# A rebuilt opening for a three-block network: shift by TensorE, x in eight pieces, four small loads on ScalarE's queue

## The chip, the cores and the metric

The kernel is one program on one core of a Trainium2 chip. The metric is the device time of one execution in microseconds (us). The kernel before took 3019.31 us as the median of three runs (3010.18 to 3040.72).

## The reference

A token matrix x (512 tokens x 1024) goes through two layers of a conditioned block and then a third block. The change is in the first microseconds of the first layer:

```
mod = silu(c) @ w_ada[0] + b_ada[0]            # c: 1 x 1024, w_ada: 1024 x 6144
sh1, sc1, g1, sh2, sc2, g2 = split(mod, 6)     # 1024 values each
h = rmsnorm(x, mix_norm[0]) * (1 + sc1) + sh1
proj = h @ w_in                                # q, k, v: 3 x 1024 columns, forget gate: 16 columns
q = rmsnorm(q per head, q_norm);  k = rmsnorm(k per head, k_norm)
log_f = log_sigmoid(f_logit + b_f);  cum = cumsum(log_f)
attention with logits + cum[t] - cum[s], output projection, x = x + g1 * y, then a mixture of experts
```

rmsnorm divides each token by the root of its mean square and multiplies by a gain. The first projection needs all 1024 features of h, so it needs sh1 and sc1, and with them 2 x 1024 columns of w_ada: 8.4 MB of weights.

## The kernel before

x is held with features on the 128 partitions: x[:, c, :] is feature block c (of 8) for all 512 tokens. Products of high precision are made from pairs: a tensor is rounded to a high part (whi, h_hi) on ScalarE, the remainder (wlo, h_lo) is formed on VectorE or GpSimd, and three matmuls (lines 124 to 126) add up hi*hi, hi*lo and lo*hi. weight (line 108) loads a 128x1024 block of weights on SyncE's queue and makes that pair; four raw blocks are kept, so the next load waits for a remainder.

The opening (first_mod, line 274) does the first modulation. The weights w_ada0 are stored transposed, so that one block of 128x1024 gives 128 entries of mod: it is multiplied by silu(c), which stands in all 128 partitions, and summed along the row. The generator ada (line 156) does that for the sixteen blocks of scale and shift, alternating scale c and shift c: ten on VectorE in one instruction (line 182), six as a multiply on GpSimd (line 179) and a summing copy on ScalarE (line 168). Beside it ScalarE squares the eight blocks of x (line 285), VectorE adds the squares (line 287), four matmuls with a column of ones sum over the partitions (line 211), VectorE forms the inverse root (lines 139 to 144), and four matmuls spread it over the partitions (line 197). Then, block by block, VectorE makes a = (1 + scale) * gain and the scaled tile n_t = x * a * r (line 299), and spread (line 236) adds the shift and makes h_hi and h_lo, on changing engines.

After it, rope_tables (line 564) makes a table of sines, and fox_heads (line 449) runs the projections: groups of 24 matmuls of 256 columns into one of two accumulators, each followed by a square on ScalarE (qk_sq) and by a row sum and the multiplication with the gain of q or k on VectorE (qk_ss, qk_raw). fox_cum (line 403) runs beside the first group: 24 matmuls for the forget gate, then a chain on ScalarE. The other 32 column blocks of mod follow as work on the side (ada again), one by one beside the attention. A scheduler puts the instructions of each engine in an order before the program runs, by its own estimates; each engine then goes through its list strictly in that order and waits where an input is missing. [...]

Of the kernel before, what the change touches and what calls it, by code (L numbers as in the profile page):

```python
# [25 lines left out]
class Net:  # L26
# [247 lines left out]
    def first_mod(self, x, gain, c, w, mod, hp, pool):  # L274

        nc = self.nc
        V = nc.vector
        h = [hp.tile([128, 8, 512], F32R, tag=n, bufs=1, name=n) for n in ("h_hi", "h_lo")]
        self.ring = pool
        ada = self.ada(c, w, mod, [k for c in range(8) for k in (8 + c, c)], "VVSVVSVS", 8, 1)  # L280
        mod, _ = mod
        acc = pool.tile([128, T], F32, name="n_acc")
        for c in range(8):
            q = pool.tile([128, T], F32, tag="n_sq", bufs=3, name="n_sq") if c else acc
# [8 lines left out]
        for c in range(8):
            for _ in range(2):
                next(ada, None)
            a = self.small([128, 1], "fm_a", bufs=4)
            V.scalar_tensor_tensor(a, mod[:, 8 + c:9 + c], 1.0, gain[:, c:c + 1], op0=OP.add, op1=OP.mult)
            t = pool.tile([128, T], F32, tag="n_t", bufs=3, name="n_t")
            V.scalar_tensor_tensor(t, x[:, c, :], a, rb, op0=OP.mult, op1=OP.mult)
            self.spread(t, mod[:, c:c + 1], h[0][:, c, :], h[1][:, c, :], c)  # L300
        self.ring = None
        return h
# [100 lines left out]
    def fox_cum(self, h, cq, ck, room, keep):  # L403
# [45 lines left out]
    def fox_heads(self, h, oT, keep, pool):  # L449
# [3 lines left out]
        gq = pool.tile([128, 64], F32, name="fox_gq")  # L453
        gk = pool.tile([128, 64], F32, name="fox_gk")
        nc.sync.dma_start(out=gq, in_=A["fox_q_norm"].to_broadcast([128, 64]))
        nc.sync.dma_start(out=gk, in_=A["fox_k_norm"].to_broadcast([128, 64]))
# [1851 lines left out]
```

## Time and profile before

| | us |
|---|---|
| median of three runs | 3019.31 |
| lowest, highest | 3010.18, 3040.72 |
| profiled execution | 3015.39 |
| its span | 3013.6 |
| TensorE busy | 2731.0 (91%) |
| VectorE busy | 2345.1 (78%) |
| ScalarE busy | 1388.6 (46%) |
| GpSimd busy | 1230.1 (41%) |

A timeline row gives the start of a piece of work in us, its duration in us, the engine, the line, the operation, out<-in by the program's names, shapes, the number of instructions merged in the row, and in brackets the idle time of the engine before it and what ended it. PE is TensorE, DVE VectorE, ACT ScalarE, POOL GpSimd, SPq the queue on which SyncE issues DMAs. The ends of matmuls are modelled; their starts tell their pace. A float32 matmul leaves two records. [...]

### The profile page before, as it was taken

Reading aid. Unit: us, or ns where it says so; the run is one execution under the profiler, and the core shown is the slowest. Engines: PE = TensorE matmul, PEld = TensorE weight load, DVE = VectorE, ACT = ScalarE, POOL = GpSimd, SP = SyncE. Lnnn points to the kernel's source line nnn. Section 1 sums busy time; section 2 is a strip of 40 time slices with the busy share of each in tenths; the row PEclk is TensorE's granted clock in tenths of the full one; section 3 lists DMA queues with packets and bytes.
Section 4 is the critical chain, followed back from the end, with each engine's and each line's share of the span. In section 5 each row is a group of like instructions: output and inputs, shape, how many; then the busy total and the mean of one; then the engine's idle time right before and its main releaser. Section 6 shows DMA issues by size and latency. Waiting matters only on the chain.

```text
span 3013.6 us, 42664 instructions
## 1 busy us (share of the span) xinstructions
PE 2731.0 (91%) x14989; PEld 2229.8 (74%) x14989; DVE 2345.1 (78%) x4500; ACT 1388.6 (46%) x2672; POOL 1230.1 (41%) x894
## 2 busy tenths in 40 slices
PE   2999979897889798899898899999999999999996
PEld 1887556686546566577676588999999999998885
DVE  7999457858885685677974699998588888887667
ACT  3355437734554573532333533588633333333332
POOL 3111017733211573004941245120177777774442
PEclk9999779999899799999998999999999999999998
DMA  6766159934555796321011124696699999998882
GB/s 214 247 225 223 66 190 307 344 107 130 157 165 209 227 336 210 98 67 29 4 60 58 62 91 129 208 315 245 212 369 355 351 355 361 356 335 298 267 275 99
DMA packets 235778, 629.51 MB, mean 209 GB/s; under 512 B 33340, under 2 KB 97388, under 8 KB 232088
## 3 DMA queue, kind: packets, MB, share of 16 engines
q1 hardware_dynamic: 135856, 436.51, 42.8%
q0 software_dynamic: 45120, 154.42, 14.6%
q10 hardware_dynamic: 54568, 35.66, 4.0%
q8 instruction: 122, 2.00, 0.3%
q14 instruction: 112, 0.92, 0.1%
HBM read 565.93 MB, written 64.36 MB: 209 GB/s over the span
## 4 chain that ended last, share of the span: by engine, by line
PE 48%; DVE 13%; DMA 2%; issue 1%; ACT 1%; POOL 0%; POOLq 0%; SPq 0%; DVEq 0%; ACTq 0%
PE acc L124 7%; PE acc L125 7%; PE acc L126 7%; PE y L126 6%; PE y L125 6%; PE y L124 6%; DVE s_y L1375 1%; PE S L1930 1%; PE tr L1930 1%; DMA wraw<-in_moe_w_gu_dram 1%; DVE wlo L118 1%; DVE s_y L1534 1%; DMA wraw<-in_moe_w_dn_dram 1%; DVE wc L1558 1%; DVE t L1782 1%
## 5 line engine op out<-in xcount | busy, mean ns | idle before, releaser
L118 DVE TENSOR_TENSOR wlo<-wraw,whi 128x1024 fp32r<-128x1024 f32 x442 | 618.7, 1410 | 198.4 <-ACT whi L117 194.0
L117 ACT ACTIVATE whi<-wraw 128x1024 fp32r<-128x1024 f32 (+1 forms) x552 | 576.9, 1050 | 411.6 <-PE acc L125 246.3
L124 PE MATMUL acc<-h_hi,whi 128*128 128x384 f32 (+1 forms) x1328 | 476.5, 359 | 12.1 <-ACT z_out L1970 8.4
L126 PE MATMUL acc<-h_hi,wlo 128*128 128x384 f32 (+1 forms) x1328 | 467.1, 352 | 2.4 <-DVE wlo L118 2.4
L125 PE MATMUL acc<-h_lo,whi 128*128 128x384 f32 (+1 forms) x1328 | 468.3, 353 | 0.0
L118 POOL TENSOR_TENSOR wlo<-wraw,whi 128x1024 fp32r<-128x1024 f32 (+1 forms) x110 | 277.5, 2530 | 317.3 <-ACT whi L117 309.9
L126 PE MATMUL y<-whi,hid_l 128*128 128x512 f32 x768 | 302.3, 394 | 0.0
L125 PE MATMUL y<-wlo,hid_h 128*128 128x512 f32 x768 | 301.0, 392 | 0.0
L124 PE MATMUL y<-whi,hid_h 128*128 128x512 f32 x768 | 298.0, 388 | 0.0
L2002 POOL DMA_INDIRECT gu<-in_peer_u_dram,e x128 | 197.3, 1541 | 240.6 <-DVE gu L2011 168.0
L124 PEld LDWEIGHTS acc<-h_hi,whi 128*128 128x128 f32 x1328 | 251.9, 190 | 29.8 <-ACT z_out L1970 9.2
L126 PEld LDWEIGHTS acc<-h_hi,wlo 128*128 128x128 f32 x1328 | 251.1, 189 | 17.1 <-DVE wlo L118 3.0
L125 PEld LDWEIGHTS acc<-h_lo,whi 128*128 128x128 f32 x1328 | 251.7, 190 | 15.7 <-issue 0.8
L2002 POOL DMA_INDIRECT gv<-in_peer_v_dram,e x128 | 201.6, 1575 | 143.0 <-DVE stage L1935 105.6
L2067 ACT ACTIVATE hid_h<-hid 128x384 fp32r<-128x384 f32 x128 | 67.3, 526 | 286.2 <-PE y L125 261.8
L2043 DVE SCALAR_TENSOR_TENSOR y<-gv,pz,y 128x1024 f32<-128x1024 f32 x128 | 189.0, 1476 | 0.0
L182 DVE SCALAR_TENSOR_TENSOR ada_w<-ada_w,silu 128x1024 f32<-128x1024 f32 x138 | 176.4, 1278 | 7.2 <-DMA ada_w<-in_w_ada_dram 7.1
L125 PEld LDWEIGHTS y<-wlo,hid_h 128*128 128x128 f32 x768 | 144.2, 188 | 31.1 <-DVE wlo L118 0.3
L124 PEld LDWEIGHTS y<-whi,hid_h 128*128 128x128 f32 x768 | 144.1, 188 | 29.6
L126 PEld LDWEIGHTS y<-whi,hid_l 128*128 128x128 f32 x768 | 144.3, 188 | 28.9
L124 PE MATMUL acc<-whi,h_hi 128*128 128x256 f32 x480 | 140.3, 292 | 26.6 <-ACT whi L117 18.7
L2011 DVE SCALAR_TENSOR_TENSOR gu<-gu,hrow 128x1024 f32<-128x1024 f32 x128 | 156.7, 1226 | 0.0
(671 smaller groups left out, 6205.8 us busy)
## 6 DMA issues: line engine op xcount, KB each, us to landing
ada_w<-in_w_ada_dram SPq DMA_DIRECT2D x144, 512.0 KB
wraw<-in_moe_w_gu_dram SPq DMA_DIRECT2D x128, 512.0 KB
wraw<-in_peer_ut_dram SPq DMA_DIRECT2D x128, 512.0 KB
wraw<-in_peer_v_dram SPq DMA_DIRECT2D x128, 512.0 KB
wraw<-in_moe_w_dn_dram SPq DMA_DIRECT2D x64, 512.0 KB
p_gd<-stage SPq DMA_DIRECT2D x24, 1024.0 KB
gt<-p_gd ACTq DMA_DIRECT2D x16, 1536.0 KB
wraw<-in_fox_w_in_dram SPq DMA_DIRECT2D x24, 512.0 KB
```

The costliest lines, as they stand in the source:

```text
L117: nc.scalar.activation(hi[:, :w], r[:, :w], AF.Copy)
L118: self.low = eng.tensor_tensor(lo[:, :w], r[:, :w], hi[:, :w].bitcast(F32), op=OP.subtract).ins
L124: mm(out=out, lhsT=l[0], rhs=r[0], start=start, stop=False)
L125: mm(out=out, lhsT=l[0], rhs=r[1], start=False, stop=False)
L126: mm(out=out, lhsT=l[1], rhs=r[0], start=False, stop=stop)
L182: V.scalar_tensor_tensor(r, r, 1.0, c, op0=OP.mult, op1=OP.mult, accum_out=m)
L1375: V.scalar_tensor_tensor(acc[:, c, :], *tap(n), acc[:, c, :], op0=OP.mult, op1=OP.add)
L1930: nc.tensor.matmul(out=pt[:, t * 128:(t + 1) * 128], lhsT=a2[:, b * 4 + t, :], rhs=a1[:, b * 4 + t, :], start=True, stop=True)
L2002: nc.gpsimd.indirect_dma_start(out=u, out_offset=None, in_=src[:, :], in_offset=bass.IndirectOffsetOnAxis(ap=e3[:, k:k + 1], axis=0))
L2011: V.scalar_tensor_tensor(u, u, 1.0, hrow, op0=OP.mult, op1=OP.mult, accum_out=z8[b][:, k % 8:k % 8 + 1])
L2043: V.scalar_tensor_tensor(y3, vs.pop(k), z8[k // 8][:, k % 8:k % 8 + 1], y3, op0=OP.mult, op1=OP.add)
L2067: nc.scalar.activation(hh, hid, AF.Copy)
```

## The change

The opening is written anew.

- The shift is computed on TensorE. Its eight weight blocks are stored untransposed, 128 inputs on the partitions and 1024 outputs in the row; c also comes as a column tile (c_col, 128x8), and two float32 matmuls per block of 512 columns each (line 311 of the new kernel) add up the whole shift in one row of two accumulators S. ScalarE copies the row (line 360), eight transposes turn it into columns (line 363), one addition gives all eight shift columns (line 364).
- The scale stays a product with a row sum on VectorE, all eight blocks now (line 314); ScalarE adds the bias and makes a.
- The squares of x are summed on TensorE, eight float32 matmuls with a column of ones (line 326); the row goes through ScalarE (line 333) and four transposes (line 336).
- x is loaded in eight pieces between the weight blocks. Shift blocks have four buffers, scale blocks six.
- The eight scaled tiles are all kept, and h_hi and h_lo of all blocks are made at the end, on ScalarE and VectorE alone.
- The first two weight blocks of the q projection are asked for in the opening (self.opened), ahead of the two small loads of the sine table.
- The gains of q and k, the forget gate's weights and its bias (fox_loads) are loaded on ScalarE's queue at the very start, no longer on SyncE's queue behind the first weight blocks.

```diff
     def first_mod(self, x, gain, c, w, mod, hp, pool):
...
-        ada = self.ada(c, w, mod, [k for c in range(8) for k in (8 + c, c)], "VVSVVSVS", 8, 1)
...
-            nc.scalar.activation(q, x[:, c, :], AF.Square)
-            if c:
-                V.tensor_tensor(acc, acc, q, op=OP.add)
...
-        r = self.rms(x, pool, acc)
+        cc = pool.tile([128, 8], F32, name="c_col")
+        nc.scalar.dma_start(out=cc, in_=A["c_col"])
+        nc.scalar.activation(cc, cc, AF.Silu)
+        ws = {}
+
+        def load(i):
+            ws[i] = pool.tile([128, D], F32, tag="ada_sc" if i >= 8 else "ada_sh", bufs=6 if i >= 8 else 4, name="ada_w")
+            nc.sync.dma_start(out=ws[i], in_=w[i])
+
+        def part(c):
+            nc.sync.dma_start(out=x[:, c, :], in_=A["x"][:, c, :])
+
+        rest = [(load, i) for k in range(8) for i in (k, 8 + k)]
+        order = rest[:4] + [(part, k) for k in range(4)] + rest[4:6] + [(part, k) for k in range(4, 8)] + rest[6:]
...
+        issue(14)
...
+        def shift(k):
+            for b in range(2):
+                mm(out=row[b][0:1, :], lhsT=cc[:, k:k + 1], rhs=ws[k][:, b * 512:(b + 1) * 512], start=k == 0, stop=k == 7)
+
+        def scale(k):
+            V.scalar_tensor_tensor(ws[8 + k], ws[8 + k], 1.0, c, op0=OP.mult, op1=OP.mult, accum_out=t8[:, k:k + 1])
+            e = slice(8 + k, 9 + k)
+            nc.scalar.activation(mod[:, e], t8[:, k:k + 1], AF.Identity, bias=bias[:, e])
...
+            nc.scalar.activation(a[k], mod[:, e], AF.Identity, scale=gain[:, k:k + 1], bias=gain[:, k:k + 1])
+
+        for k in range(2):
+            shift(k)
+            scale(k)
+        for k in range(8):
+            q = pool.tile([128, T], F32, tag="n_sq", bufs=3, name="n_sq")
+            nc.scalar.activation(q, x[:, k, :], AF.Square)
+            mm(out=sq[0:1, :], lhsT=self.ones, rhs=q, start=k == 0, stop=k == 7)
+            if k == 3:
+                shift(2)
+                scale(2)
+                issue(4)
...
+        nc.scalar.activation(srow, sq[0:1, :], AF.Copy)
...
+            nc.tensor.transpose(st[:, i:i + 1], srow[:, i * 128:(i + 1) * 128], self.ident[:1, :1])
...
+        for k in range(4, 8):
+            issue(2)
+            shift(k)
+            scale(k)
+            scaled(k - 4)
+        self.opened = [self.weight(A["fox_w_in"][k]) for k in range(2)]
+        for k in range(4, 8):
+            scaled(k)
...
+            nc.scalar.activation(shr[:, b * 512:(b + 1) * 512], row[b][0:1, :], AF.Copy)
...
+            nc.tensor.transpose(pt[:, k:k + 1], shr[:, k * 128:(k + 1) * 128], self.ident[:1, :1])
+        V.tensor_tensor(mod[:, 0:8], pt[:, 0:8], bias[:, 0:8], op=OP.add)
+        for k in range(8):
+            self.spread(ts[k], mod[:, k:k + 1], h[0][:, k, :], h[1][:, k, :], 0)
         return h
...
-        nc.sync.dma_start(out=wf, in_=A["fox_w_f"])
-        nc.sync.dma_start(out=bf, in_=A["fox_b_f"])
...
+    def fox_loads(self, room, keep):
...
+        for t, a in ((gq, A["fox_q_norm"].to_broadcast([128, 64])), (gk, A["fox_k_norm"].to_broadcast([128, 64])),
+                     (wf, A["fox_w_f"]), (bf, A["fox_b_f"])):
+            nc.scalar.dma_start(out=t, in_=a)
...
-        nc.sync.dma_start(out=x, in_=A["x"])
...
+    o["w_ada0"][:8] = i["w_ada"][0][:, :1024].reshape(8, 128, 1024)
+    o["c_col"] = cols(i["c"].reshape(-1))
```

SyncE's list at the start, before (silu is c in all partitions, ada_w a block of w_ada, wraw a block of the projection, oT the room that holds the forget gate's weights and bias):

```order
L152 DMA silu<-in_c_dram 128x1024
L2174 DMA x<-in_x_dram 128x4096
L174 DMA ada_w<-in_w_ada_dram 128x1024 x16
L569 DMA r_pi<-in_positions_dram 128x4
L571 DMA r_fr<-in_inv_freq_dram 128x16
L105 DMA wraw<-in_fox_w_in_dram 128x1024 x2
L409 DMA oT<-in_fox_w_f_dram 128x128
L410 DMA oT<-in_fox_b_f_dram 16x1
L105 DMA wraw<-in_fox_w_in_dram 128x1024 x6
L455 DMA fox_gq<-in_fox_q_norm_dram 128x64
```

and now:

```order
L152 DMA silu<-in_c_dram 128x1024
L289 DMA ada_w<-in_w_ada_dram 128x1024 x4
L292 DMA x<-in_x_dram 128x512 x4
L289 DMA ada_w<-in_w_ada_dram 128x1024 x2
L292 DMA x<-in_x_dram 128x512 x4
L289 DMA ada_w<-in_w_ada_dram 128x1024 x10
L105 DMA wraw<-in_fox_w_in_dram 128x1024 x2
L644 DMA r_pi<-in_positions_dram 128x4
L646 DMA r_fr<-in_inv_freq_dram 128x16
L105 DMA wraw<-in_fox_w_in_dram 128x1024 x6
```

x has moved between the blocks, the two weight blocks stand ahead of the sine table's loads, and the four small loads have left the list.

TensorE's list at the start, before (n_acc is the sum of the squares, acc the accumulators, n_r_y the inverse root):

```order
L211 MATMUL misc<-ones,n_acc 128x1 x4
L197 MATMUL acc<-ident,n_r_y 128x128 x4
L124 MATMUL acc<-whi,h_hi 128x256
L125 MATMUL acc<-wlo,h_hi 128x256
L126 MATMUL acc<-whi,h_lo 128x256
```

and now (S holds the shift row, tr the row of sums, sh_row its copy):

```order
L311 MATMUL S<-ada_w,c_col 1x512 x4
L326 MATMUL tr<-n_sq,ones 1x512 x4
L311 MATMUL S<-ada_w,c_col 1x512 x2
L326 MATMUL tr<-n_sq,ones 1x512 x4
L311 MATMUL S<-ada_w,c_col 1x512
L336 MATMUL misc<-ident,s_row 128x1 x4
L311 MATMUL S<-ada_w,c_col 1x512 x3
L197 MATMUL acc<-ident,n_r_y 128x128 x4
L311 MATMUL S<-ada_w,c_col 1x512 x6
L363 MATMUL misc<-ident,sh_row 128x1 x8
L124 MATMUL acc<-whi,h_hi 128x256
L124 MATMUL acc<-h_hi,fox_wfh 16x512
```

The sixteen shift matmuls and eight row sums have come in front, and the forget gate's matmuls (fox_wfh, fox_wfl) have moved from behind the first projection group into it.

ScalarE's list around the forget gate's chain (oT) and the first squares of q, before:

```order
L117 ACTIVATE whi<-wraw 128x1024 x2
L592 ACTIVATE cos<-r_r 128x64
L592 ACTIVATE sin<-r_r 128x64
L467 ACTIVATE qk_sq<-acc 128x256
L418 ACTIVATE oT<-acc,oT 16x512
L419 ACTIVATE oT<-oT 16x512
L420 ACT_TABLE_LOAD
L420 ACTIVATE oT<-oT 16x512
L421 ACT_TABLE_LOAD
L421 ACTIVATE oT<-oT 16x512
L467 ACTIVATE qk_sq<-acc 128x256 x2
```

and now:

```order
L240 ACTIVATE h_hi<-n_t,mod_113 128x512 x7
L117 ACTIVATE whi<-wraw 128x1024 x2
L481 ACTIVATE oT<-acc,oT 16x512
L482 ACTIVATE oT<-oT 16x512
L667 ACTIVATE cos<-r_r 128x64
L667 ACTIVATE sin<-r_r 128x64
L483 ACT_TABLE_LOAD
L483 ACTIVATE oT<-oT 16x512
L542 ACTIVATE qk_sq<-acc 128x256 x2
L484 ACT_TABLE_LOAD
L484 ACTIVATE oT<-oT 16x512
```

The first square of q (qk_sq) has moved from ahead of the forget gate's chain into its middle, behind the first table load, and the seven h_hi follow each other.

From the third group of k in the first quarter on, the lists of all five engines are the same in both kernels.

## Rows read from the trace of the kernel before

**Rows 1.** The page, part 1: busy us, share of the span, instructions.
```profile
PE 2731.0 (91%) x14989; PEld 2229.8 (74%) x14989; DVE 2345.1 (78%) x4500; ACT 1388.6 (46%) x2672; POOL 1230.1 (41%) x894
```

**Rows 2.** Stretches: from:to, length, busy us (instructions) by engine, TensorE's granted clock, DMA.
```profile
50.00:57.00 7.00, 0.00 (x0) 0.00 (x0) 7.00 (x15) 3.23 (x5) 3.82 (x2) 1.00 0.00 0
...
150.00:200.00 50.00, 49.94 (x369) 41.05 (x368) 46.27 (x128) 26.36 (x64) 6.18 (x6) 1.00 0.69 232
```

**Rows 3.** TensorE's timeline, 60 to 71 us: start, duration, engine, line, operation, idle before.
```profile
60.30 0.58 PE L125 MATMUL acc<-wlo,h_hi 128*128 128x256 f32 x1 [2.44 <-DVE wlo L118]
...
63.46 0.41 PE L124 MATMUL acc<-whi,h_hi 128*128 128x256 f32 x1
63.67 0.38 PE L125 MATMUL acc<-wlo,h_hi 128*128 128x256 f32 x1
...
64.12 0.28 PE L125 MATMUL acc<-wlo,h_hi 128*128 128x256 f32 x1
64.24 0.28 PE L126 MATMUL acc<-whi,h_lo 128*128 128x256 f32 x1
...
70.05 0.40 PE L126 MATMUL acc<-h_hi,fox_wfl 128*16 128x512 f32 x1
```

**Rows 4.** VectorE's timeline, 23 to 74 us.
```profile
23.05 3.37 DVE L182 SCALAR_TENSOR_TENSOR ada_w<-ada_w,silu 128x1024 f32<-128x1024 f32 x1
...
33.01 0.16 DVE L252 TENSOR_SCALAR n_v<-misc 128x4 f32<-128x4 f32 x1 [1.70 <-PE misc L211]
...
36.23 0.16 DVE L144 SCALAR_TENSOR_TENSOR n_r_y<-n_r_z,n_r_y 128x4 f32<-128x4 f32 x1
...
59.03 1.21 DVE L118 TENSOR_TENSOR wlo<-wraw,whi 128x1024 fp32r<-128x1024 f32 x1
...
60.17 0.74 DVE L241 SCALAR_TENSOR_TENSOR h_lo<-n_t,mod,h_hi 128x512 fp32r<-128x512 f32 x1
...
73.30 0.42 DVE L469 TENSOR_TENSOR qk_raw<-acc,fox_gq 128x256 f32<-128x256 f32 x1 [4.18 <-DMA fox_gq<-in_fox_q_norm_dram]
```

**Rows 5.** SyncE's timeline, 0 to 69 us: the issue of DMAs.
```profile
1.73 34.03 SPq L174 DMA_DIRECT2D ada_w<-in_w_ada_dram  x16
...
38.18 1.99 SPq L410 DMA_DIRECT2D oT<-in_fox_b_f_dram  x1
...
68.30 0.38 SPq L455 DMA_DIRECT2D fox_gq<-in_fox_q_norm_dram  x1
```

**Rows 6.** Stretches of the opening, for the last column, the DMA's GB/s.
```profile
0.00:10.00 10.00, 0.00 (x0) 0.00 (x0) 3.83 (x5) 2.34 (x2) 7.07 (x22) 1.00 0.81 285
...
10.00:20.00 10.00, 0.00 (x0) 0.00 (x0) 6.91 (x11) 3.74 (x7) 2.61 (x1) 1.00 1.02 362
...
16.00:18.00 2.00, 0.00 (x0) 0.00 (x0) 2.00 (x3) 0.29 (x1) 1.58 (x1) 1.00 1.03 422
```

**Rows 7.** ScalarE's timeline, 5 to 64 us.
```profile
5.75 1.06 ACT L153 ACTIVATE silu<-silu 128x1024 f32<-128x1024 f32 x1 [3.21 <-DMA silu<-in_c_dram]
...
11.22 0.63 ACT L285 ACTIVATE n_acc<-x 128x512 f32<-128x512 f32 x1 [4.41 <-DMA x<-in_x_dram]
...
57.80 0.72 ACT L240 ACTIVATE h_hi<-n_t,mod 128x512 fp32r<-128x512 f32 x1
...
61.88 1.99 ACT L117 ACTIVATE whi<-wraw 128x1024 fp32r<-128x1024 f32 x2
```

**Rows 8.** TensorE's timeline, 1577 to 1588 us, in a later layer norm.
```profile
1577.58 1.92 PE L1670 MATMUL S<-s_y,cent 128*128 128x512 f32 x2
...
1579.42 3.59 PE L1226 MATMUL acc<-n_sq,ones 128*1 128x512 f32 x8
...
1586.65 0.40 PE L1232 MATMUL misc<-ident,n_row 1*128 1x1 f32 x4
```

**Rows 9.** The stretch ahead of those matmuls.
```profile
1574.00:1579.00 5.00, 4.99 (x6) 1.85 (x6) 1.73 (x3) 0.45 (x1) 0.00 (x0) 0.50 0.96 343
```

**Rows 10.** All instructions of line 1228: duration min/median/max, first and last start, forms.
```profile
L1228 ACT ACTIVATE n_row<-acc x4: 374/374/571, 1217.3 to 1684.5; 1x256 f32<-1x256 f32 x3, 1x512 f32<-1x512 f32 x1
```

More of the change, by code (lines that the diff above doesn't have):

```diff
@@ L274, in first_mod @@
     def first_mod(self, x, gain, c, w, mod, hp, pool):
-        nc = self.nc
+        nc, A = self.nc, self.A
         V = nc.vector
+        mm = nc.tensor.matmul
         h = [hp.tile([128, 8, 512], F32R, tag=n, bufs=1, name=n) for n in ("h_hi", "h_lo")]
-        self.ring = pool
-        ada = self.ada(c, w, mod, [k for c in range(8) for k in (8 + c, c)], "VVSVVSVS", 8, 1)
[L281 to L284, printed above, removed]
-            nc.scalar.activation(q, x[:, c, :], AF.Square)
-            if c:
-                V.tensor_tensor(acc, acc, q, op=OP.add)
-            if c >= 2:
-                next(ada)
@@ new lines, in first_mod, with issue @@
+        rest = [(load, i) for k in range(8) for i in (k, 8 + k)]
+        order = rest[:4] + [(part, k) for k in range(4)] + rest[4:6] + [(part, k) for k in range(4, 8)] + rest[6:]
+        order = iter(order)
+        def issue(n):
+            for f, k in itertools.islice(order, n):
+                f(k)
+        row = [self.psum(t, 2) for t in ("S", "S")]
+        sq = self.psum("tr", 2)
+        a, ts = {}, {}
+        first = []
+        issue(14)
+        t8 = pool.tile([128, 8], F32, name="fm_t")
@@ new lines, in first_mod @@
+        for k in range(2):
[9 more added lines that the diff above has]
+                issue(4)
+        issue(1)
+        srow = pool.tile([1, T], F32, name="s_row")
+        nc.scalar.activation(srow, sq[0:1, :], AF.Copy)
@@ L291, in first_mod @@
+        st = self.psum("misc", 1)
+        for i in range(4):
+            nc.tensor.transpose(st[:, i:i + 1], srow[:, i * 128:(i + 1) * 128], self.ident[:1, :1])
+        v = self.small([128, 4], "n_v4")
+        V.tensor_scalar(v, st[:, 0:4], 1.0 / D, 1e-6, op0=OP.mult, op1=OP.add)
+        issue(1)
+        shift(3)
+        scale(3)
+        r = self.rsqrt(v, 4, "n_r4")
         rb = self.psum("acc", 2)
         self.bcast_cols(rb, r)
[L293 to L300, printed above, removed]
@@ L301, in first_mod, with scaled @@
-        self.ring = None
+        def scaled(k):
+            ts[k] = pool.tile([128, T], F32, tag="n_t", bufs=8, name="n_t")
+            V.scalar_tensor_tensor(ts[k], x[:, k, :], a[k], rb, op0=OP.mult, op1=OP.mult)
+        for k in range(4, 8):
[6 more added lines that the diff above has]
+            scaled(k)
+        shr = pool.tile([1, D], F32, name="sh_row")
@@ L302, in first_mod @@
+        for b in range(2):
+            nc.scalar.activation(shr[:, b * 512:(b + 1) * 512], row[b][0:1, :], AF.Copy)
+        pt = self.psum("misc", 1)
+        for k in range(8):
+            nc.tensor.transpose(pt[:, k:k + 1], shr[:, k * 128:(k + 1) * 128], self.ident[:1, :1])
+        V.tensor_tensor(mod[:, 0:8], pt[:, 0:8], bias[:, 0:8], op=OP.add)
+        for k in range(8):
+            self.spread(ts[k], mod[:, k:k + 1], h[0][:, k, :], h[1][:, k, :], 0)
         return h
@@ L452, in fox_heads @@
         ck = keep.tile([128, 4, 512], BF16, name="f_ck")
[L453 to L456, printed above, removed]
+        gq, gk = gains
         def quart(quart, ready):
@@ L459, in quart @@
             for which, g in ((0, gq), (1, gk)):
-                ws = [self.weight(A["fox_w_in"][(4 * which + quart) * 2 + k]) for k in range(2)]
+                if quart == 0 and which == 0:
+                    ws = self.opened
+                else:
+                    ws = [self.weight(A["fox_w_in"][(4 * which + quart) * 2 + k]) for k in range(2)]
                 raw = pool.tile([128, 4, 4, 64], F32, tag="qk_raw", bufs=4, name="qk_raw")
```

13 lines of the change are left out of this document (11 added, 2 removed).

## The prediction

> **What bounds the kernel now.** I began with the page's table of engines: TensorE is busy 91% of the span [rows 1], so time is lost only where TensorE stands still. The busy times by stretch show where that is: in the 7 us from 50 to 57 TensorE does nothing while VectorE is busy 7.00 of 7.00 us; from 150 to 200 TensorE is busy 49.94 of 50 [rows 2]. The opening is thus a VectorE stage with an idle TensorE behind it, and what follows is a TensorE stage that starts when the opening lets it. TensorE's timeline gives the start: the projections run from 60.30 us, and the last forget-gate product is done at 70.05 + 0.40 = 70.45 us [rows 3]. VectorE's timeline shows why so late: seven adds for the row sums, ten of the sixteen 128x1024 products and all the normalizing stand in one queue, and some are stretched: an operation on 128x1024 takes 1.21 us alone, and a product took 3.37 while GpSimd worked on its own [rows 4]. The DMA is not the limit there: the sixteen weight blocks were asked for until 35.8 us [rows 5] only because buffers came free late.
>
> **Does it reach the end?** From the third k group of the first quarter on, the order of instructions on all five engines is the same in both kernels, row for row. From 150 us TensorE is full [rows 2], so an opening that ends d us earlier moves everything behind it by d. I find no transfer or clock time that stands still while the rest moves.
>
> **What goes.** The seven adds, the eight shift products (VectorE and GpSimd), GpSimd's six long multiplies and four h_lo, and ScalarE's accumulating copies leave the opening. All of it was in front of TensorE, and its place is what the terms below replace. VectorE's remaining products should run at the undisturbed 1.2 us, since GpSimd is empty there.
>
> **What comes, step by step.**
> 1. *Loads.* Up to the last shift block the queues carry 0.52 (c) + 2.10 (x) + 15 x 0.524 (blocks) + 0.39 (small ones) = 10.9 MB. Before, 285 GB/s x 10 us + 362 x 10 = 6.5 MB had moved at 20 us, and 422 GB/s was reached [rows 6]. The new order asks for the same bytes at least as densely (x in eight pieces, shift blocks freed by TensorE), so the other 4.4 MB at about 415 GB/s take 10.6 us: 30.6 us. x was usable at 11.22 us [rows 7], about 1 us after its 2.9 MB had passed; so the last shift block is usable at 31.6 us, the last scale block 1.3 us later. [...]
> 2. *TensorE's new work.* 16 shift matmuls and 8 row-sum matmuls, float32, 512 columns, one output row. [...] TensorE can start near 7.5 us: silu ran at 5.75 for 1.06 us [rows 7], and ScalarE now issues five small DMAs ahead of its table load. At the upper clock 21.6 us fit between 7.5 and 31.6 and the loads set the end; I take this, since the work is dense from the first blocks on: at 60.30, too, TensorE began low, worked without a gap, and by 64.12 started a matmul of 256 columns every 0.12 us where it had been 0.21 [rows 3].
> 3. *From the last shift block to the first h.* Two matmuls 1.8, copy of the second half-row 0.57 [rows 10], eight transposes 0.80 (four took 0.40 [rows 8]), one add 0.16: 35.0 us. The inverse root is ready long before: it needs x alone, and its VectorE chain took 36.23 + 0.16 - 33.01 = 3.4 us [rows 4], hidden by the loads.
> 4. *The eight h.* h_hi[0] 0.72 [rows 7]: 35.7. Then on VectorE eight h_lo and the last scaled tile at 0.74, and two weight remainders at 1.21 [rows 4]: 9.1 us, so 44.8 us. ScalarE's seven h_hi and two weight roundings (1.99 for two [rows 7]) lie beside it.
> 5. *First projection.* TensorE now mixes the first group (24 matmuls of 256 columns) with 24 forget-gate matmuls while the h arrive. [...] It begins at about 37, low as at 60.30, rises on the way, and has some 3 us left after the last h_lo: done at 48.0 us.
> Against 70.45 that is **22.4 us earlier**.
> 6. *The four small loads.* Before, the query gain was asked for at 68.30 [rows 5], behind weight loads that wait for buffers, and VectorE stood 4.18 us for it until 73.30 [rows 4], but TensorE had a second accumulator to go on with. Now the gain is there in the first microseconds and ScalarE pays the issues; the one-column bias held its queue for 1.99 us before [rows 5], and ScalarE is idle until silu anyway. Part of the removed wait comes back: ScalarE now has the first square of q behind the forget gate's chain, where it stood ahead of it. I price the two together at nothing, between 2 us gained and 2 lost.
>
> **The sum.** 3015.4 (the profiled execution; its span of 3013.6 and 1.8 around it) - 22.4 = 2993. The median of the three runs is 3.9 us above that execution; I put half of that on top: **2995 us**, 0.7 to 0.8% faster. On its own this forecast spans a gain of 16 to 28 us.
>
> **The rivals.**
> - *The clock stays low on the new matmuls* (15%). For it: they come in pairs that wait for loads, and the trace has 0.50 at just such single float32 matmuls [rows 8, 9]. Against it: the row sums right behind them ran at the upper clock [rows 8]. Price: 24 x 1.84 = 44 us from 7.5, plus the broadcast (four of 128 columns, a quarter of 1.84 each) and low transposes, 3 to 4 us, so TensorE and no longer the loads sets the end; shift row ready at 55, and steps 3 to 5 add 13: 68, a gain of 2 to 3 us, 3013. [...]
> - *Slower: the low clock also holds through the first projections* (8%). Then TensorE stays low into the mixed forget-gate products (15 us instead of 8.4, step 5) and the three query groups after them (24 x 0.09 us more each, 6.5 in all), which ran at the upper clock before because everything was ready for them. 68 + 7 + 6 is 10 us past today's point: 3025. It decides where the projections of the second group still start 0.21 us apart.
> - *The load queue stalls on the small transfers* (10%). [...] The query gain took from 68.30 to 73.30, 5 us, to land in traffic [rows 4, 5]. If all five take that long, one behind another on ScalarE's queue, the stream thins for up to 8 us around 5 to 13 us: gain 14, 3003. Against it: nothing else is under way at 1 us.
> - *More than I count* (5%). The end of the opening comes when the loads end and step 4 overlaps better, or the crowded first groups behind it close up since their loads come earlier: gain 32, 2985.
> My forecast has the remaining 62%.
>
> **Numbers.** Below 2982 lie half of the last rival and little else, above 3015 the slower one and some of the low-clock one: the range is 2982 to 3015, some 8 in 10. About 1% (30 us) is what a measurement of this kernel can tell from no change, its three runs being 30 us apart. Faster by more than 1% means below 2989: a part of my own range (13%) and most of the last rival, 18%. Slower by over 1% is 3%; the rest, 79%, is within 1%.
>
> **What would show it.** In the changed profile: the last shift matmul ends at 33 to 34 us (step 1, 2); its pairs last 1.8 us, not 3.6 (clock); the last forget-gate product ends at 48 (70.45 now); VectorE waits for no gain; GpSimd is empty until the first head. From the third projection on, every mark stands 20 to 24 us earlier, and the shift is the same at 200 us as at the end. I am wrong if the opening ends that early and the end does not move, if the sixteen blocks take over 36 us to land, or if the shift pairs stay at the low clock.

## The result and the profile after

The changed kernel takes 3002.52 us (median of 19 runs, 2994.91 to 3013.51); the kernel before, on the same chip, 3017.05 (19 runs). The medians differ by 14.5 us (0.5%). The ratio, formed from the single runs and not from the medians, is 0.994, 95% interval 0.9926 to 0.9954: some 0.6% faster, a gain clear of the noise but small. One run before, at 4482.76 us, and one of e4 below, at 11772.95, are not in the ratios. The profiled execution took 3002.52 us, its span is 3000.8, against 3013.6 before.

The page, part 1, answers [rows 1]: VectorE and GpSimd are relieved, and TensorE has 27 us more work, the slow float32 matmuls of the opening among it (3.60 us for four row sums).

```profile
PE 2758.3 (92%) x15041; PEld 2227.4 (74%) x15041; DVE 2316.6 (77%) x4466; ACT 1385.8 (46%) x2680; POOL 1211.1 (40%) x884
```

The opening by stretches, with the columns of [rows 2]; it answers [rows 2, 6].

```profile
0.00:10.00 10.00, 1.95 (x3) 0.34 (x4) 4.27 (x6) 2.55 (x3) 5.12 (x22) 1.00 0.84 178
10.00:20.00 10.00, 7.93 (x10) 0.88 (x9) 2.61 (x5) 3.51 (x8) 0.00 (x0) 1.00 0.99 383
20.00:30.00 10.00, 10.00 (x28) 2.17 (x27) 2.87 (x8) 3.36 (x7) 0.00 (x0) 1.00 1.03 406
30.00:40.00 10.00, 7.32 (x23) 1.89 (x20) 8.83 (x21) 2.69 (x9) 0.00 (x0) 1.00 0.95 368
40.00:50.00 10.00, 6.62 (x26) 4.49 (x27) 9.04 (x14) 9.00 (x16) 0.00 (x0) 0.67 0.36 109
50.00:57.00 7.00, 6.23 (x34) 3.86 (x33) 5.56 (x21) 2.39 (x4) 0.00 (x0) 0.98 0.50 164
150.00:200.00 50.00, 50.00 (x377) 42.53 (x377) 46.20 (x126) 27.22 (x66) 6.25 (x7) 1.00 0.67 219
```

VectorE, busy 9.90 of the 10 us from 20 to 30 before, is now idle for 7 of them, while TensorE is full. The loads start thin, 178 GB/s against 285. From 50 to 57 TensorE works, where it stood still.

TensorE's timeline answers [rows 3, 8]: first the shift pairs (S) and the row sums (tr), then the row's transposes and the first projection.

```profile
8.05 3.57 PE L311 MATMUL S<-ada_w,c_col 128*1 128x512 f32 x4 [8.05 <-ACT c_col L284]
13.69 3.57 PE L311 MATMUL S<-ada_w,c_col 128*1 128x512 f32 x4 [2.07 <-DMA ada_w<-in_w_ada_dram]
...
21.75 1.88 PE L311 MATMUL S<-ada_w,c_col 128*1 128x512 f32 x4
23.46 3.60 PE L326 MATMUL tr<-n_sq,ones 128*1 128x512 f32 x8
...
31.69 1.16 PE L197 MATMUL acc<-ident,n_r_y 128*128 128x128 f32 x8 [0.77 <-DVE n_r_y L144]
32.78 5.31 PE L311 MATMUL S<-ada_w,c_col 128*1 128x512 f32 x12
40.57 0.88 PE L363 MATMUL misc<-ident,sh_row 1*128 1x1 f32 x8 [2.48 <-ACT sh_row L360]
44.18 0.58 PE L124 MATMUL acc<-whi,h_hi 128*128 128x256 f32 x1 [2.73 <-ACT whi L117]
...
55.41 0.39 PE L126 MATMUL acc<-h_hi,fox_wfl 128*16 128x512 f32 x1
```

The last shift matmul ends at 38.09, the last forget-gate product at 55.80, where [rows 3] have 70.45: **14.65 us earlier**. Before the last six shift matmuls stands the broadcast of the inverse root (n_r_y), and TensorE waited 0.77 us for that root; otherwise it had work without a gap from 17.05 to 38.09.

VectorE's timeline answers [rows 4]: the root's first and last step, the scaled tile that waits for ScalarE, the last scale product, the addition that gives the shift columns, and the first use of the gain.

```profile
28.29 0.16 DVE L338 TENSOR_SCALAR n_v<-misc 128x4 f32<-128x4 f32 x1 [6.85 <-PE misc L336]
...
31.48 0.16 DVE L144 SCALAR_TENSOR_TENSOR n_r_y<-n_r_z,n_r_y 128x4 f32<-128x4 f32 x1
...
40.07 0.75 DVE L348 SCALAR_TENSOR_TENSOR n_t<-x,fm_a,acc 128x512 f32<-128x512 f32 x1 [0.78 <-ACT fm_a L318]
40.73 1.22 DVE L314 SCALAR_TENSOR_TENSOR ada_w<-ada_w,silu 128x1024 f32<-128x1024 f32 x1
...
41.88 0.16 DVE L364 TENSOR_TENSOR mod<-misc,bias 128x8 f32<-128x8 f32 x1
...
59.71 0.42 DVE L543 TENSOR_REDUCE qk_ss<-qk_sq 128x4 f32<-128x256 f32 x1 [4.15 <-ACT qk_sq L542]
60.05 0.41 DVE L544 TENSOR_TENSOR qk_raw<-acc,fox_gq 128x256 f32<-128x256 f32 x1
```

The products run at 1.22 us. Between the root's last step and the addition VectorE makes four scale products and seven scaled tiles, 10.40 us with 0.96 us idle. No gain is waited for, but 4.15 us for the square of q, which ScalarE makes behind the forget gate's chain.

SyncE's issues, and the waits behind them (queue and line, what it waited for, us in total, times, longest), answer [rows 5].

```profile
1.27 5.96 SPq L289 DMA_DIRECT2D ada_w<-in_w_ada_dram  x4
7.28 3.57 SPq L292 DMA_DIRECT2D x<-in_x_dram  x4
10.89 1.81 SPq L289 DMA_DIRECT2D ada_w<-in_w_ada_dram  x2
13.66 2.96 SPq L292 DMA_DIRECT2D x<-in_x_dram  x4
16.97 13.07 SPq L289 DMA_DIRECT2D ada_w<-in_w_ada_dram  x10
...
SPq L289 <- PE S L311: 6.1, 2, 4.7
SPq L289 <- DMA bias<-in_b_ada_dram: 3.6, 1, 3.6
```

Four weight blocks took 5.96 us to ask for. One of them waited 3.6 us for the bias, an earlier small load, to land. The second half of x was asked for at 13.66 and later. The 6.1 us of waiting for shift matmuls (S), which free the shift blocks' four buffers, did not thin the loads: by the completion events of the trace the blocks behind x landed every 1.3 us, the last shift block at 34.40 and the last scale block at 35.68.

### The profile page after: what moved, and what is told of

Its sections match the earlier page's. It is cut to its first block, busy times and chain, and to the rows that moved or that the text cites. A ratio compares the mean times of both kernels' runs of the same rounds, so it can differ in the third digit from the quotient of the medians.

```text
span 3000.8 us, 42742 instructions
## 1 busy us (share of the span) xinstructions
PE 2758.3 (92%) x15041; PEld 2227.4 (74%) x15041; DVE 2316.6 (77%) x4466; ACT 1385.8 (46%) x2680; POOL 1211.1 (40%) x884
## 3 DMA queue, kind: packets, MB, share of 16 engines
q8 instruction: 123, 2.02, 0.3%
## 4 chain that ended last, share of the span: by engine, by line
PE 50%; DVE 11%; DMA 3%; issue 1%; ACT 1%; POOL 0%; POOLq 0%; DVEq 0%; ACTq 0%; SPq 0%
PE acc L124 7%; PE acc L126 7%; PE acc L125 7%; PE y L125 6%; PE y L126 6%; PE y L124 6%; DMA wraw<-in_moe_w_gu_dram 2%; PE tr L2006 1%; PE S L2006 1%; DMA wraw<-in_moe_w_dn_dram 1%; DVE s_y L1451 1%; DVE s_y L1610 1%; DVE wlo L118 1%; DVE t L1858 1%; DVE sys_x L1612 1%
## 5 line engine op out<-in xcount | busy, mean ns | idle before, releaser
L118 DVE TENSOR_TENSOR wlo<-wraw,whi 128x1024 fp32r<-128x1024 f32 x442 | 626.3, 1427 | 199.6 <-ACT whi L117 194.6
L182 DVE SCALAR_TENSOR_TENSOR ada_w<-ada_w,silu 128x1024 f32<-128x1024 f32 x128 | 162.0, 1266 | 4.5 <-DMA ada_w<-in_w_ada_dram 4.2
```

What stands on the lines that cost most here:

```text
L118: self.low = eng.tensor_tensor(lo[:, :w], r[:, :w], hi[:, :w].bitcast(F32), op=OP.subtract).ins
L182: V.scalar_tensor_tensor(r, r, 1.0, c, op0=OP.mult, op1=OP.mult, accum_out=m)
```

## The experiments

The times of before beside the four groups of runs: 3018.01 (27 runs), 3019.39 (15), 3018.03 (29), 3015.17 (15). Ratios are to these, the changed kernel's to the 19 runs above; they too are formed from the single runs. The column of the last h_lo is VectorE's: in the kernel before and in e1 GpSimd ends one later, at 63.76 and 65.54. The last column is the end of the last forget-gate product. The intervals of e2, e3, e4, e6, e7, e9, e11, e12 and e13 all overlap with the changed kernel's: the times tell only e1, e8 and e14 from it, and what follows rests on the marks, each from one trace.

| run | us | ratio (95%) | last shift end | last h_lo | forget gate |
|---|---|---|---|---|---|
| before | | 1 | - | 60.91 | 70.45 |
| changed | 3002.52 | 0.994 (0.9926-0.9954) | 38.09 | 51.25 | 55.80 |
| e1 | 3018.18 | 1.0015 (0.9993-1.0036) | - | 62.59 | 71.43 |
| e2 | 3003.67 | 0.996 (0.9939-0.998) | 35.71 | 48.87 | 55.58 |
| e3 | 3005.80 | 0.9958 (0.9943-0.9973) | - | 52.29 | 57.13 |
| e4 | 3004.37 | 0.995 (0.9933-0.9966) | 36.87 | 49.96 | 53.85 |
| e8 | 3012.05 | 0.9974 (0.9955-0.9994) | - | 51.77 | 61.84 |
| e9 | 3007.72 | 0.9952 (0.9931-0.9973) | - | 48.90 | 58.80 |
| e12 | 3008.22 | 0.9957 (0.9937-0.9978) | - | 53.17 | 58.96 |
| e11 | 3003.12 | 0.9935 (0.9916-0.9954) | 37.53 | 49.02 | 52.54 |
| e7 | 3003.33 | 0.993 (0.9908-0.9952) | 38.38 | 51.55 | 55.15 |
| e6 | 3004.47 | 0.9954 (0.9937-0.9971) | 37.02 | 49.25 | 54.55 |
| e13 | 3007.10 | 0.9961 (0.9945-0.9977) | 38.48 | 48.50 | 51.94 |
| e14 | 3011.82 | 0.9984 (0.997-0.9998) | 39.41 | 49.43 | 52.42 |

### Which part carries the gain

**e1: the old opening, only the four small loads moved to ScalarE's queue.**

```diff
+                    gains = self.fox_loads(oT[:, 2:8], ph)
                     h = self.first_mod(x, gain, c, ...)
```


> The old opening with one part of the change: the four small loads (gains of q and k, forget gate's weights and bias) at the start of ScalarE's queue. Theory A (the gain comes from the rebuilt opening; the small loads only remove a wait that TensorE did not feel, and hold up the first big loads): the wait of 4.18 us for the query gain is gone, the last forget-gate product still ends at 70 to 72 us (70.45 before), the time is that of before within 3 us. Rival B (the small loads bring a part of the gain by themselves): that product is no later and the time falls by 4 us or more.

No gain: 3018.18, forget gate at 71.43, though VectorE no longer waits for the gain. That wait was worth nothing on the path.

**e2: the new opening, the four small loads back on SyncE's queue, where they were.**

```diff
-                    gains = self.fox_loads(oT[:, 2:8], ph)
...
+        nc.sync.dma_start(out=gq, in_=A["fox_q_norm"].to_broadcast([128, 64]))
```


> The new opening with the four small loads back on SyncE's queue where they were. [...] Rival B (the early small loads are worth more than they cost): the time is 3 us or more above the change's. Rival C (TensorE, not the loads, sets the end of the shift): the blocks come earlier and the last shift matmul still ends at 37.5 to 38.5.

The first four blocks are asked for in 1.96 us instead of 5.96 and the shift ends 2.38 us earlier. The forget gate does not come earlier (its own weights come later), and VectorE waits 5.13 us for the gain. The early loads cost 2.4 us in the stream and give as much back.

**e3: the shift as products on VectorE again, all else new.**

```diff
-            for b in range(2):
-                mm(out=row[b][0:1, :], lhsT=cc[:, k:k + 1], rhs=ws[k][:, b * 512:(b + 1) * 512], ...)
+            V.scalar_tensor_tensor(ws[k], ws[k], 1.0, c, op0=OP.mult, op1=OP.mult, accum_out=...)
```


> The new opening with one part undone: the shift is again a product with a row sum per block on VectorE (weights transposed as before), so TensorE has only the eight row sums and the broadcast. Theory A (in the change TensorE's own chain, 16 shift matmuls partly at the low clock, the shift row's copies and transposes, ends the opening, while VectorE is idle for most of 10 to 30 us): VectorE takes the eight products in its idle time, the first h are made while the last blocks land, the last forget-gate product ends at 50 to 53 us (55.8 in the change) and the time falls by 2 to 6 us more. Rival B (the gain came from taking products off VectorE): VectorE becomes the bound again, that product ends at 58 to 63, and the time is 3 to 7 us above the change's.

57.13: the shift on TensorE is worth 1.3 us. Neither theory gave that number; the gain had to be elsewhere, so I built it up from the old opening.

**e8: the old opening with GpSimd empty.**

```diff
-        ada = self.ada(c, w, mod, [...], "VVSVVSVS", 8, 1)
+        ada = self.ada(c, w, mod, [...], "V", 8, 1)
...
-            self.spread(t, mod[:, c:c + 1], h[0][:, c, :], h[1][:, c, :], c)
+            self.spread(t, mod[:, c:c + 1], h[0][:, c, :], h[1][:, c, :], 0)
```


> The opening of before with one thing changed: its sixteen products are all on VectorE and no h_lo on GpSimd, so GpSimd is empty in the opening. Theory 1 (VectorE lost time to GpSimd): in the opening of before some ten operations of VectorE are stretched by 1 to 2.2 us each beside GpSimd's multiplies, some 15 us in all; VectorE takes on six products of 1.21 and four h_lo of 0.74 and loses four adds of 0.48, 8.4 us more, so the last h_lo comes 5 to 7 us earlier and the last forget-gate product at 64 to 66 (70.45 before): 3010 to 3012 us against 3017. Theory 2 (the queue's length decides): 8 us more work on the engine that was busy without a gap, forget gate at 74 to 79, 3022 to 3026 us.

VectorE has more to do and ends its h_lo at 51.77 instead of 60.91: the forget gate comes 8.6 us earlier, more than theory 1 said. In e8 all products take 1.22 us, as this one; the 3.37 of [rows 4] is gone:

```profile
23.37 1.22 DVE L182 SCALAR_TENSOR_TENSOR ada_w<-ada_w,silu 128x1024 f32<-128x1024 f32 x1
```

**e9: e8, and the row sums on TensorE.**

```diff
-                V.tensor_tensor(acc, acc, q, op=OP.add)
+            nc.tensor.matmul(out=sq[0:1, :], lhsT=self.ones, rhs=q, start=c == 0, stop=c == 7)
```


> As the run before (old opening, GpSimd empty), and the row sums of the squares of x on TensorE, eight matmuls with a column of ones, in place of seven adds on VectorE. Theory 1 (VectorE's queue is what the opening waits for): seven adds of 0.68, 4.8 us, leave it and the root comes earlier, forget gate 4 to 6 us ahead of the run before, at 59 to 61, 3005 to 3008 us; then the rest of the new opening (x in pieces, the order, h at the end) is worth the 2 to 4 us that are left to the 57.1 of the version with all products on VectorE. Theory 2 (the gain is in the order of the new opening, h at the end and its loads): within 2 us of the run before.

Another 3.0 us, 58.80. In its trace the h are ready earlier than in the changed kernel (48.90 against 51.25), and TensorE and VectorE then wait, here for the first weight remainder and there for the gain:

```profile
48.28 0.58 PE L125 MATMUL acc<-wlo,h_hi 128*128 128x256 f32 x1 [7.07 <-DVE wlo L118]
...
60.40 0.42 DVE L475 TENSOR_TENSOR qk_raw<-acc,fox_gq 128x256 f32<-128x256 f32 x1 [4.83 <-DMA fox_gq<-in_fox_q_norm_dram]
```

**e12: e9, the small loads early (GpSimd's queue), the first two projection blocks asked for in the opening.**

```diff
+            if c == 3:
+                self.opened = [self.weight(self.A["fox_w_in"][k]) for k in range(2)]
```


> The old opening with GpSimd empty and the row sums on TensorE (its last forget-gate product stood at 58.8 us, its last h_lo at 48.9), and two more things of the new one: the four small loads at the start (on GpSimd's queue) and the first two projection blocks asked for within the opening. The shift stays on VectorE and x comes in one piece. Theory 1 (what was left of the gain lay in these two: TensorE stood 7.1 us for the first weight remainder, VectorE 4.8 us for the gain): forget gate at 53 to 56, no wait for a gain, 2999 to 3003 us, as fast as the change without the shift on TensorE. Theory 2 (the shift on TensorE and h at the end are needed to get there): forget gate at 57 to 59, 3004 to 3007 us.

Theory 2: the wait for the gain goes and TensorE starts on the first remainder 5 us earlier (43.30), yet the forget gate stays at 58.96. The weight remainders now stand between the h in VectorE's list, and its last h_lo moves to 53.17.

The ladder of the 14.65 us, in this order of the steps: GpSimd emptied 8.6 (70.45 to 61.84), sums on TensorE 3.0 (58.80), the new order with x in pieces and early loads 1.7 (e3, 57.13), shift on TensorE 1.3 (55.80).

### What set the end of the opening

**e4: 18 idle matmuls ahead of the first shift pair, 14 behind it.**

```diff
+                mm(out=idle, lhsT=self.ones_b, rhs=self.ones_b[:, None, :].to_broadcast([128, 4, 128]), ...)
```


> The change with 18 idle matmuls of 512 columns (bf16, ones) ahead of the first shift pair and 14 between the first and the second, to a tile that nobody reads; nothing else moves. Theory A (the low clock of the first pairs, 3.57 us for two matmuls each instead of 1.8, sits in the chain that ends the shift): the pairs take 1.8 us, the last shift matmul ends 2 to 4 us earlier than 38.1, the last forget-gate product 2 to 4 us earlier than 55.8, the time falls by as much. Rival B (the loads set the end): the pairs are faster, and the last shift matmul still ends at 37.5 to 38.5, the time stays.

The first two pairs take 1.88 us, no longer 3.57. The last shift matmul gains 1.2 us and the forget gate 2.0: the slow pace of two pairs was a small part of the loss. Theory A's direction came out, not its 2 to 4 us at the shift's end: there the loads now set it, since the last shift block landed at 34.95 and its matmuls end 1.92 us later.

**e7: the small loads on GpSimd's queue.**

```diff
-            nc.scalar.dma_start(out=t, in_=a)
+            nc.gpsimd.dma_start(out=t, in_=a)
```


> The changed kernel with the four small loads on GpSimd's queue in place of ScalarE's. [...] Theory 2 (the root, which hangs on the second half of x, sets the pace): the blocks come earlier but the second half of x does not, last shift matmul within 1 us of 38.1, forget gate 55 to 56, 3002 to 3003 us.

The four blocks are asked for in 2.02 us, 5.96 in the changed kernel: the long wait among them came with the small loads on ScalarE's queue. The last shift matmul still ends at 38.38, as theory 2 said. The lead in the loads did not last: with the four small loads under way on GpSimd's queue, 126 GB/s were moved from 10 to 12 us and 224 from 12 to 14, 298 and 407 in the changed kernel, which differs in their queue alone. So x came no sooner: the first row sum starts at 16.91, 17.05 in the changed kernel and 15.54 in e2.

**e11: x ahead of the sixteen blocks.**

```diff
-        order = rest[:4] + [(part, k) for k in range(4)] + rest[4:6] + [(part, k) for k in range(4, 8)] + rest[6:]
+        order = [(part, k) for k in range(8)] + rest
```


> The new opening, with all eight pieces of x asked for ahead of the sixteen weight blocks (in the changed kernel four blocks, four pieces, two blocks, four pieces). Theory 1, the inverse root sets the pace: in the changed kernel the second half of x lands at 21 to 24 us, the row sums are done at 27.1, the root at 31.6, and six of the sixteen shift matmuls and all scaled tiles are queued behind it. With x first the squares run from 8 to 14 us, the sums are done by 16 and the root by 21 to 24, and the loads set the end again: last shift matmul at 34 to 36 (38.1 now), last forget-gate product at 51 to 53.5 (55.8), 2999 to 3001 us. Theory 2, TensorE's own matmuls set it (low clock on the first pairs): the eight row sums only change places with shift pairs, the first pair runs low as before, last shift matmul at 37.5 to 39, forget gate at 55 to 57, 3002 to 3004 us. Theory 3, VectorE's eight scale products now start 6 us later behind x and become the bound: last scale product still at 41 to 43, forget gate at 55.8 or later.

In TensorE's list the row sums now also stand ahead of all shift pairs. Its timeline:

```profile
24.56 1.16 PE L197 MATMUL acc<-ident,n_r_y 128*128 128x128 f32 x8
25.65 7.03 PE L311 MATMUL S<-ada_w,c_col 128*1 128x512 f32 x16
33.09 1.88 PE L311 MATMUL S<-ada_w,c_col 128*1 128x512 f32 x4 [0.41 <-DMA ada_w<-in_w_ada_dram]
35.65 1.88 PE L311 MATMUL S<-ada_w,c_col 128*1 128x512 f32 x4 [0.69 <-DMA ada_w<-in_w_ada_dram]
```

The root comes 7 us earlier, the broadcast waits for nothing, and the forget gate is at 52.54, where theory 1 put it. The last shift matmul is not (37.53, 34 to 36 expected): now its block is waited for. It landed at 35.61: the loads of the first 10 us moved only 165 GB/s, and SyncE later waited 10.5 us for shift matmuls to free buffers (351 GB/s from 20 to 30 us, 406 in the changed kernel). The time, 3003.12, is above theory 1's 2999 to 3001.

**e6: each scale block ahead of its shift block.**

```diff
-        rest = [(load, i) for k in range(8) for i in (k, 8 + k)]
+        rest = [(load, i) for k in range(8) for i in (8 + k, k)]
```


> The changed kernel with each pair of weight blocks in the other order, the scale block ahead of the shift block. Theory 1 (the shift row is ready at 38.1 us, but ScalarE's and VectorE's lists hold it up: the row's copies wait until 39.94 behind the a of the seventh scale block, the addition until 41.88 behind the eighth scale product): scale work ends about 1.3 us earlier, the last shift matmul at 38 to 39, the addition at 40 to 41 (41.88 now), the last forget-gate product at 54 to 55 (55.8). Theory 2 (the last block loaded decides, whichever it is): the shift block is now the last one, its matmuls end 1.3 us later at 39.4, the addition at 41.5 to 42, forget gate unchanged at 55.5 to 56. Time 3001 to 3004 us by either: a difference of 1 us in the time is less than these runs can tell, the marks decide.

The forget gate gains 1.25 us, as theory 1 has it, but by another way: the row's second copy (41.05) and the addition (42.32) come even later, behind a weight rounding and a weight remainder, and the h_lo behind them are denser.

**e13: x in one piece first, scale's small steps on VectorE, GpSimd's queue, 36 idle matmuls.**

```diff
+            nc.sync.dma_start(out=x, in_=A["x"])
...
+            V.tensor_tensor(mod[:, e], bias[:, e], t8[:, k:k + 1], op=OP.add)
+            V.scalar_tensor_tensor(a[k], mod[:, e], 1.0, gain[:, k:k + 1], op0=OP.add, op1=OP.mult)
```


> The changed kernel put right where its trace lost time: x in one piece right behind c and ahead of the blocks (the loads of its first 10 us moved 178 GB/s, 285 before), the small loads on GpSimd's queue, the two scalar steps of each scale block on VectorE (it waited 0.78 us a block for ScalarE), and 36 idle matmuls on TensorE until x is there (so that the row sums find the upper clock). Theory 1 (with these the loads set the end, as forecast for the change): over 270 GB/s in the first 10 us, row sums done by 17 to 18 us, the root by 22, last shift matmul at 33 to 35 (38.1 now), last h_lo at 44.5 to 47, last forget-gate product at 47.5 to 50 (55.8), 2994 to 2999 us. Theory 2 (VectorE's own work behind the root, scale products and scaled tiles in one list, sets it): last scale product at 38 or later, last h_lo at 48 to 50, forget gate at 51.5 to 54, 2999 to 3002 us.

289 GB/s in the first 10 us, and still theory 2's marks (h_lo 48.50, forget gate 51.94). c's column, 4 KB, asked for at 1.25, held ScalarE until 10.98; the shift blocks' four buffers then held the loads (SyncE waited 10.4 us for shift matmuls).

```profile
10.98 0.21 ACT L284 ACTIVATE c_col<-c_col 128x8 f32<-128x8 f32 x1 [7.95 <-DMA c_col<-in_c_col_dram]
```

Two more table loads in ScalarE's order (1.28 us each in the changed kernel), ahead of the first square of q, put the first gain product at 59.88, no earlier than in the changed kernel. The time, 3007.10, lies in neither theory's range.

**e14: e13 with six shift buffers, c's column first, the sine table made during the loads.**

```diff
-bufs=6 if i >= 8 else 4
+bufs=6 if i >= 8 else 6
...
+                    self.cs = self.rope_tables(self.xp, pre)
                     h = self.first_mod(...)
```


> As the run before (x in one piece behind c, small loads on GpSimd's queue, scalar steps of the scale on VectorE, 36 idle matmuls), with three things mended that its trace shows: six buffers for shift blocks in place of four (there the fifth shift block waited until 20.5 us for the first shift matmul, which stood behind the row sums, and the loads moved 291 GB/s from 10 to 20 us), c's column asked for first on ScalarE's queue (it landed at 10.9 us, and silu and the squares stood behind it), and the sine table made during the loads (its two table switches held the first square of q until 58.8 us). Theory 1 (the forecast's own chain, loads that never wait and then 9 us of h): at 30 us 10.4 MB or more have landed, last shift matmul at 33 to 35 us, first h at 36 to 37.5, last h_lo at 44.5 to 47, last forget-gate product at 47.5 to 50, the first gain multiplied at 49 to 52 (60.05 in the changed kernel, 59.88 in the run before), 2993 to 2998 us, 5 to 9 faster than the change. Theory 2 (an opening that ends earlier brings no more, what is won is lost in the first heads or behind them): the same marks up to 52 us, but 3001 to 3004 us, as all versions so far whose forget gate stood between 52 and 57.

The first gain product is at 50.89, as theory 1 said. The last shift matmul is not at 33 to 35: SyncE waited 5.1 us for the bias to land, the loads moved 277 GB/s from 10 to 20 us, and the root was late again, with steps of the sine table and scale products ahead of its chain and in it on VectorE:

```profile
27.02 1.16 PE L197 MATMUL acc<-ident,n_r_y 128*128 128x128 f32 x8 [3.35 <-DVE n_r_y L144]
28.11 11.30 PE L318 MATMUL S<-ada_w,c_col 128*1 128x512 f32 x22
```

And the time is worse than the changed kernel's, 3011.82. The 128 exponentials of the softmax line (durations, first and last start) show when the lead is lost; the changed kernel:

```profile
L387 ACT ACTIVATE P<-S,sm_mx x128: 363/530/715, 112.2 to 888.5; 128x128 f32<-128x128 f32 x32, 128x256 f32<-128x256 f32 x32, 128x384 f32<-128x384 f32 x32, 128x512 f32<-128x512 f32 x32
```

and e14:

```profile
L384 ACT ACTIVATE P<-S,sm_mx x128: 363/532/711, 106.2 to 887.4; 128x128 f32<-128x128 f32 x32, 128x256 f32<-128x256 f32 x32, 128x384 f32<-128x384 f32 x32, 128x512 f32<-128x512 f32 x32
```

It is 6.0 us ahead at the first and 1.1 at the last. What follows is lost later, in a stage in which TensorE never stands still. The stretch from 2200 to 2700 us, of the changed kernel:

```profile
2200.00:2700.00 500.00, 500.00 (x2513) 451.55 (x2513) 423.59 (x482) 176.09 (x252) 375.19 (x254) 1.00 0.97 353
```

of before:

```profile
2200.00:2700.00 500.00, 500.00 (x2538) 455.34 (x2537) 428.30 (x487) 178.72 (x255) 375.29 (x257) 1.00 0.99 356
```

and of e14:

```profile
2200.00:2700.00 500.00, 500.00 (x2489) 451.55 (x2488) 420.28 (x478) 174.52 (x249) 369.12 (x251) 1.00 0.97 350
```

The work is the same, the granted clock too, and TensorE has no idle time, but it did 2538, 2513 and 2489 matmuls; VectorE's counts differ in the same proportion (487, 482, 478), so it is not a matter of records that are missing. e2, e3, e4, e6, e7, e11 and e13 have 2512 to 2515, but e1 and e12, with most of the old opening, have 2511 as well, e9 2524 and e8 2492. 24 matmuls in 500 us are 4.8 us. So the pace in a stage that no edit touched differs between these traces by up to 2%, and not by old or new opening. Whether it goes with the kernel or with the execution is open, since each kernel has one trace; executions of the changed kernel lie 18.6 us apart. Theory 2 of e14 thus holds in its first half (the lead is lost behind the heads), and not in its number. No version is measurably faster than the changed kernel.

## Why the prediction was right, and where its chain failed

Forecast 2995, range 2982 to 3015, no change within 1% at 0.79: the time is 3002.5, inside. The direction was right, and so was the first half of the mechanism: TensorE starts earlier because the opening is no longer a full VectorE beside a busy GpSimd. What carried it is less the work that VectorE lost than the stretching that it lost (a product of 3.37 us beside GpSimd's work, 1.22 in e8): e8 gave it more to do, emptied GpSimd and has 8.6 of the 14.65 us, and the shift on TensorE brought 1.3. The opening gained 14.65 us where the sum had 22.4, so the chain of the sum failed.

- **Step that failed: 3, "the inverse root is ready long before".** The sum let x land as early as it did before. In the new order its second half comes behind six weight blocks, so the row sums end at 27.06 us and the root's last step starts at 31.48. Behind it VectorE still has four scale products and seven scaled tiles, which the sum priced at nothing but for one tile; only then does it add the shift (41.88). The row's copies wait too, until 39.94, behind the a of the seventh block, which comes out of the same list. The addition stands 10.40 us behind the root's last step in the changed kernel, and again in e2 and e7 (below) and e4 (10.41, 30.18 to 40.59), though their last shift matmuls end at 35.71, 38.38 and 36.87. It ends at 42.04 where the sum had 35.0: 7.0 of the 7.8 us by which 48.0 was missed. The root's last step and the addition, in e2 and then in e7:

```profile
29.09 0.16 DVE L144 SCALAR_TENSOR_TENSOR n_r_y<-n_r_z,n_r_y 128x4 f32<-128x4 f32 x1
39.49 0.16 DVE L364 TENSOR_TENSOR mod<-misc,bias 128x8 f32<-128x8 f32 x1
```

```profile
31.77 0.16 DVE L144 SCALAR_TENSOR_TENSOR n_r_y<-n_r_z,n_r_y 128x4 f32<-128x4 f32 x1
42.17 0.16 DVE L364 TENSOR_TENSOR mod<-misc,bias 128x8 f32<-128x8 f32 x1
```

- e11, x first, has the root's last step 7.3 us earlier (24.18), but the addition only 2.2 (39.65) and the forget gate 3.3. Behind the root VectorE's list then has six scale products in place of four and four waits of 0.78 us for ScalarE's a, and the addition again comes right behind the eighth product. That is theory 3 of e11, with an end at 39.7 and not 41 to 43.
- **Step 2, "the loads set the end", failed as well, for the shift row.** The last shift matmul ends at 38.09 instead of 33.4, 4.7 us late. Its block landed 2.8 us late (34.40, 31.6 forecast); the other 1.9 us are TensorE's own list, which was busy 20.23 of the 21 us from 17 to 38 and waited 0.77 for the root. In e4, e6, e11 and e13 the last shift matmul ends 1.92 us behind the landing of its block, so there the loads do set it.
- **Step 1, loads as dense as before, failed too**: 178 GB/s in the first 10 us. That was my third rival, a load queue held up by small transfers. It had a gain of 14 and 3003 us, and both came out; but the held queue explains a third of the miss at most. With the queue free the root came 2.4 us earlier in e2 and 0.3 us later in e7. The right number stood there with a third of the right cause: that is luck. What the trace shows of such a queue is the 3.6 us wait for the bias; why a weight block waits for another load no run shows. The 415 GB/s that the sum put on the rest of the loads was not far off: 406 from 20 to 30 us.
- **Step 2's clock**: the first two pairs took 3.57 us, later ones 1.88; in e4, behind 18 and 14 idle matmuls, the first two took 1.88 as well. So the low-clock rival was right for two pairs and part of the first row sums (4.86 us for four, 3.59 in e4), and wrong for the rest; price 1.2 us at the shift's end (e4). That the slower pace is a lower clock is my reading: the granted clock's column reads 1.00 there. The 21.6 us of step 2 are 24 float32 matmuls at 0.90 us, the 1.8 of step 3 two of them, both from 3.59 us for four, and the rival's 1.84 us is the time between two starts [rows 8].
- **Step 4** was right: from the addition to the last h_lo 9.8 us forecast (35.0 to 44.8), 9.2 measured (42.04 to 51.25). **Step 5** had 3.2 us behind the last h_lo and took 4.6; the granted clock was 0.67 from 40 to 50, though no run shows that alone to be the reason. The second rival's 15 and 8.4 us for step 5 are an estimate, 24 matmuls of 256 columns at 0.21 or 0.12 us [rows 3] and 24 of 512 at twice that; from start to start, 256 and 512 columns took 0.21 and 0.43 us near 45 us here, 0.12 and 0.23 near 51. The three differences, 7.0 - 0.6 + 1.4, make the 7.8 us between 48.0 and 55.80.
- **Step 6** was right: e1 changes nothing, and the 4.18 us wait for the gain has become 4.15 us for ScalarE.
- **"The shift is the same at 200 us as at the end"** was wrong, and so was the claim that nothing stands still: 14.6 us at the first softmax exponential, 17.5 at the last (126.8 and 906.0 before), 12.8 at the end of the span. In between it is more: an instruction that VectorE starts at 2200 us before comes 21.9 us earlier now. Later stages add and take some us by a pace of their own, so that the time's gain comes out so near the opening's 14.65 us is partly luck.

## What to carry to other kernels

An input of a long chain (here x, for the root) belongs ahead of bulk weights, even if the bulk is what fills the queue: ask which list stands behind the chain's end, not only when the last byte lands. In e11 that was worth 3.3 us at the forget gate, and nothing that the time shows. When one engine's work is stretched beside another's, as VectorE's product here (3.37 us beside GpSimd's multiplies, 1.22 without), emptying the other can be worth more than giving it a share of the work: e8 gave VectorE 8 us more to do and won 8.6. And a few us at the start of a 3000 us kernel are read from marks near the edit; the total moves by as much between executions.

## What the runs showed of the hardware

- The bulk queue waited for a small load to land: 3.6 us for the bias in the changed kernel, 4.5 us for c's column in e13 and 5.1 us for the bias in e14 (SyncE's waits). Beside 2.6 MB of other loads (c and x), 4 KB took from 1.25 to 10.98 us to be usable.
- With the four small loads on GpSimd's queue (e7) the loads moved 126 and 224 GB/s from 10 to 12 and 12 to 14 us, 298 and 407 with them on ScalarE's (the changed kernel).
- The pace of TensorE at a granted clock of 1.00, without idle time, was 2489 to 2538 matmuls in the 500 us from 2200 to 2700, by trace.
- The granted clock's column reads 1.00 from 0 to 20 us in the changed kernel, where two shift pairs took 3.57 us each; later pairs took 1.88, and so did these two behind the idle matmuls of e4. Here the durations told the pace, not the column.
